# A hybrid attention, state-space and mixture-of-experts block: two places where work is put in another order

## The chip, the core and the metric

The kernel runs on one core of a Trainium2 chip. The metric is the time of one execution in microseconds (us) on the device; lower is better. The engines are TensorE (PE, matmuls; its weight loads stand apart as PEld), VectorE (DVE), ScalarE (ACT), GpSimd (POOL) and the queues from which DMAs are issued (SP, POOL and ACT). Each engine works through its own instructions in program order.

## The reference

A block takes 2048 tokens of 1024 channels and 16 meta tokens. After a LayerNorm it runs grouped-query attention (8 heads, 2 key heads, 64 wide) and a state-space layer side by side, gates and sums them, and normalizes. Then 16 experts each pick 256 tokens, work on them, and their results are added into the stream before a last LayerNorm.

```python
s = einsum('bqkgd,bskd->bkgqs', qblk, k) * scale
p = softmax(s, axis=-1)
o = einsum('bkgqs,bskd->bqkgd', p, v)
...
gate, idx = lax.top_k(softmax(logits, axis=1), cap)       # cap = 256 tokens for each expert
xe = t[idx]
h = silu(xe @ w_gate[e]) * (xe @ w_up[e])
ye = (h @ w_down[e]) * gate                               # added to the rows idx
...
h = layer_norm(alpha * h + moe, ln2_g, ln2_b)             # the output, 2048 rows
```

## The kernel before

**Attention** (`phase_b`). The work is 32 units: 4 blocks of 512 queries by 8 heads. A unit is 9 steps: 8 of 256 keys and a last one of the 16 meta keys. In a step PE makes scores (`scores`, tile `pS`), ACT takes the exponential (`pe`) and a 16-bit copy of it (`ph`, `split_hi`; for step 3 of a unit DVE makes that copy), POOL or DVE makes the 16-bit rest (`pl`, `split_lo`), and four steps later PE multiplies both with the values (`pv`, tile `po`).

The exponential needs the maximum of each row of scores beforehand. While one unit runs, PE makes plain scores of the next unit in 20 chunks of some 413 keys (`max_mm`, tile `pm`), and DVE reduces each chunk to a maximum per row (`max_red`, tile `mx`). When all 20 are reduced, `max_fin` joins them, and `max_put` has PE transpose them (four matmuls with the identity, again into a tile `pm`) and DVE copy the transposes into the rows 64 to 127 of the next unit's queries `q`. The tile `pm` has two buffers (PSUM banks). Chunks that wait for their reduction stand in the list `pend`; `red_all` reduces all of them.

What an engine does in a step follows a string, `PROG`, written out by hand: S and T are the two halves of the scores, M a chunk for the next unit, P a part of the values, and "/" means `red_all` and one item of DVE's queue. At a T the transposes are put too, where some are due:

```python
PROG=("SMTM/PPP/P/M/", "SMTMPP/PP/MM/M", "SMTM//PPPP/M/M")
```

**Experts** (`experts`). An expert is 16 steps: 8 halves of gate and up (`gate_up`, tile `pg`) and 8 of down (`down`, tile `pd`, two buffers). Weights come in pieces of 1 MB from SP's queue (tile `wr`, three buffers); ACT makes the rounded copy `wh` and DVE the rest `wl`. ACT and DVE also make the activation (`sg`, `hh`, `hl`), the transposed tokens (`xh`, `xl`) and, in the down steps, ACT moves each `pd` to `ye`. POOL's queue issues the gathers of tokens (`xg`) and the scatters that add `ye` to `acc_d` in memory.

**Final normalization.** From expert 9 on (`E0`) each step ends with `step(e, s)`, which takes every generator in `sides` one yield further. `finish` is the first of them: it loads two tiles of 128 rows of `acc_d` (`fx`, four buffers), and starts a pair of tiles every 11 steps through `norm`: sums of both tiles on ACT; one step later the mean on DVE (`fm`); then a square sum on ACT in each of two steps (`fj`, `fq`); a reciprocal root in two steps of small DVE instructions (`newton`); and four DVE steps that scale. Then POOL's queue stores the rows. `redo(e - 1)` starts in step 2 of each expert from 10 on: it gathers the rows that expert e - 1 changed (`fa`), and, five steps later, normalizes them in the same way and writes them over the output rows (`put_rows`). So `finish` and a `redo` run side by side, and in one step the job that stands first in `sides` has its instructions ahead on each engine.

Of the kernel before, what the change touches and what calls it, by code (L numbers as in the profile page):

```python
# [40 lines left out]
def row_bcast(ap, n, parts=128):  # L41
    return bass.AP(tensor=ap.tensor, offset=ap.offset, ap=[[0, parts], [1, n]])
# [7 lines left out]
def kernel(ctx, tc, x, meta, ln_in_g, ln_in_b, w_in, q_norm_g, k_norm_g,  # L50
# [326 lines left out]
    def phase_b(c):  # L377
# [61 lines left out]
        def load_q(n):  # L439
            qb, h = units[n]  # L440
            q1 = qp.tile([128, 512], F32R, name="q1", bufs=3)
            q2 = qp.tile([128, 512], F32R, name="q2", bufs=3)
            r, t0 = 64 * (h % 2), 512 * qb
            for i in range(2):
                SP.dma_start(f(q1[64 * i:64 * i + 64]), q_d[i, h // 2, r:r + 64, t0:t0 + 512])
            SP.dma_start(f(q2[:64]), q_d[0, h // 2, r:r + 64, t0:t0 + 512])
            Q[n] = q1, q2
            MX[n] = qp.tile([128, 4, 5], F32, name="mx")

        def max_mm(n, i):  # L450
            j, c = divmod(i, 5)
            k0, w = MC[c]
            p = po.tile([128, 512], F32, name="pm", bufs=2)
            PE.matmul(p[:, :w], Q[n][0][:, 128 * j:128 * j + 128], K1[units[n][1] // 4][:, k0:k0 + w],  # L454
                      start=True, stop=True)
            pend.append((n, j, c, p, w))
# [14 lines left out]
        def max_put(n):  # L471
            nm = NMT[n % 2]
            p = po.tile([128, 4, 128], F32, name="pm", bufs=2)
            for j in range(4):
                PE.matmul(p[:, j], nm[:, j], idr, start=True, stop=True)
            V.tensor_copy(Q[n][1][64:], p[64:].rearrange("p j q -> p (j q)"))  # L476

        def scores(n, i, a):
            g = units[n][1] // 4
            w = 2 if i < NT // 2 else 1  # L480
            m = 128 if i < NT // 2 else NM
            if a >= w:
                return
            if a == 0:
                PS[n, i] = ps.tile([128, 2, 512], F32, name="pS")
            p = PS[n, i]
            k0 = 128 * (2 * i + a)
            PE.matmul(p[:m, a], K2[g][:, k0:k0 + m], Q[n][1], start=True, stop=False)  # L488
            PE.matmul(p[:m, a], K1[g][:, k0:k0 + m], Q[n][0], start=False, stop=True)  # L489
            if a < w - 1:  # L490
                return
            e = pp.tile([128, 2, 512], F32, name="pe", bufs=PR["PE"]) if w == 2 else p[:, 1:]
            hi = pp.tile([128, 2, 512], F16, name="ph", bufs=PR["PH"])
            lo = pp.tile([128, 2, 512], F16, name="pl", bufs=PR["PH"])
            A.activation(e[:m, :w], p[:m, :w], AF.Exp, bias=ebias[:m], scale=HD ** -0.5)  # L495
            P[n, i] = e, hi, lo, m, w
# [5 lines left out]
        def split_hi(n, i, on_v):  # L502
            e, hi, lo, m, w = P[n, i]
            if on_v and i in PR["HI"]:
                V.tensor_reduce(hi[:m, :w], e[:m, :w, :, None], axis=AX.X, op=OP.max)  # L505
            if not on_v and i not in PR["HI"]:
                A.copy(hi[:m, :w], e[:m, :w])  # L507

        def split_lo(n, i):
            e, hi, lo, m, w = P[n, i]  # L510
            (PL if w == 2 else V).tensor_tensor(lo[:m, :w], e[:m, :w], hi[:m, :w], op=OP.subtract)  # L511
# [27 lines left out]
        def pv_fin(n):  # L539
            qb, h = units[n]  # L540
            if h == 0:
                Y[qb] = sm.tile([128, 4, 512], F32, name="y")
            y = Y[qb]
            t = O.pop(n).rearrange("p a b d -> p (a b) d")
            r = sm.tile([128, 4], F32, name="r")
            V.reciprocal(r, t[:, :, 64])
            PL.tensor_tensor(t[:, :, 0:64], t[:, :, 0:64], t[:, :, 65:129], op=OP.add)
            PL.tensor_tensor(y[:, :, 64 * h:64 * h + 64], t[:, :, 0:64],
                             r[:, :, None].to_broadcast([128, 4, 64]), op=OP.mult)
            if h == H - 1:  # L550
                PL.dma_start(y_d[512 * qb:512 * qb + 512].rearrange("(j p) d -> p j d", p=128), y)
# [6 lines left out]
        def red_all():  # L558
            while pend:
                n, j, c = pend[0][:3]  # L560
                max_red()
                if (j, c) == (3, 4):
                    max_fin(n)
                    put.append(n)
# [30 lines left out]
        for s in range(len(steps) + LAG):  # L595
            want = min(NC, int((s + LEAD) * 20 // NP))
            live = s < len(steps)
            if live:
                n, i = steps[s]
                if i == 0 and n + 2 < NU:  # L600
                    load_q(n + 2)
            if 0 <= s - PR["LOS"] < len(steps) and steps[s - PR["LOS"]][1] < NP - 1:
                split_lo(*steps[s - PR["LOS"]])
            if 0 < s <= len(steps) and steps[s - 1][1] in PR["HI"]:
                vq.insert(0, lambda st=steps[s - 1]: split_hi(*st, True))
            if fin and fin[0][0] == s:
                vq.append(lambda x=fin.pop()[1]: pv_fin(x))
            if s >= LAG:
                pvq += [(*steps[s - LAG], k) for k in range(4)]
            prog = PR["PROG"][s % len(PR["PROG"])]  # L610
            if s == len(steps) + LAG - 1:
                prog = prog.replace("P", "") + "P/" * len(pvq)
            for tok in prog:
                if tok == "M" and done < want:
                    if len(pend) == 2:
                        red_all()
                    max_mm(*chunks[done])
                    done += 1
                elif tok == "S" and live:
                    scores(n, i, 0)  # L620
                elif tok == "T":
                    if live:
                        if n and i == 0:
                            vq.pop(0)()
                        scores(n, i, 1)
                    while put:
                        max_put(put.pop())
                elif tok == "P" and pvq:
                    u, k, part = pvq.pop(0)
                    pv(u, k, part)  # L630
                    if (k, part) == (NP - 1, 3):
                        pv_out(u)
                        fin.append((s + 2, u))
                elif tok == "/":
                    red_all()
                    if vq:
                        vq.pop(0)()
            if live:
                split_hi(n, i, False)
                if i == NP - 1:  # L640
                    vq.insert(0, lambda st=steps[s]: split_lo(*st))
            if s == len(steps) - 1:
                c2.close()
            if s == len(steps) + LAG - 1:
                while vq:
                    vq.pop(0)()
            yield "tail" if s >= len(steps) else "pre" if s == len(steps) - 40 else ""
# [1033 lines left out]
    def experts(c, pos, inf):  # L1681
# [221 lines left out]
        def finish():  # L1903
            SP.dma_start(gb, row_bcast(ln2_g, D))
            SP.dma_start(bb, row_bcast(ln2_b, D))
            xs = {}

            def load(t):
                xs[t] = fp.tile([128, D], F32, name="fx", bufs=4)
                PL.dma_start(xs[t], acc_d[128 * t:128 * t + 128])  # L1910

            yield
            for t in range(2):
                load(t)
            yield
            yield

            def base(t):
                for n, _ in enumerate(norm([xs[t], xs[t + 1]])):
                    if n == 7 and t + 2 < NT:  # L1920
                        load(t + 2)
                        load(t + 3)
                    yield
                for i in range(2):
                    PL.dma_start(outs[t + i], xs.pop(t + i))

            yield from pipe((base(t) for t in range(0, NT, 2)), every=MO[3])
# [11 lines left out]
        sides = []  # L1939

        def step(e, s):
            if (e, s) == (E0, 0):
                sides.append(finish())
            if E0 < e < E - 1 and s == MO[0]:
                sides.append(redo(e - 1, MO[1]))
            if (e, s) == (E - 1, 1):
                acc_rows(e)
                sides.append(redo(e - 1, MO[2]))
            for g in sides:
                next(g, None)  # L1950

        one_hot(0, 0, NT)
# [188 lines left out]
```

## Time and profile before

| | |
|---|---|
| time, median of 3 runs | 3164.24 us (3161.82 to 3164.74) |
| profiled execution, its own time | 3164.63 us |
| its span, first to last instruction | 3162.1 us |
| PE busy | 2969.1 us (94%) |
| DVE busy | 2162.1 us (68%) |
| ACT busy | 1549.6 us (49%) |
| POOL busy | 1007.6 us (32%) |
| mean granted TensorE clock | 0.977 |

The 2.5 us between the span and its execution's time lie outside the instructions. Busy shares are means over stages: in attention ACT and POOL are nearly full, in the experts they are not.

### The profile page before, as it was taken

How to read it: one execution, taken by the hardware profiler on the slowest of the kernel's cores; microseconds unless marked ns; L12 is line 12 of the kernel's file. 1: busy time of each engine (PE TensorE's matmuls, PEld its weight loads, DVE VectorE, ACT ScalarE, POOL GpSimd, SP SyncE). 2: the span in 40 equal slices, each digit the busy share in tenths (PEclk: the TensorE clock that was granted, in tenths of full speed). 3: DMA queues.
4: the chain of work that ended last, by engine and by line, in shares of the span. 5: the costliest groups of instructions: out<-in, count | busy, mean ns of one | idle time of the engine just before them, and what ended most of it. 6: DMA issues, size and time to landing. Idle time of an engine off the chain costs nothing.

```text
span 3162.1 us, 56209 instructions
## 1 busy us (share of the span) xinstructions
PE 2969.1 (94%) x22829; PEld 2632.9 (83%) x22829; DVE 2162.1 (68%) x3760; ACT 1549.6 (49%) x2197; POOL 1007.6 (32%) x630
## 2 busy tenths in 40 slices
PE   7998999999989999999899996799999999999997
PEld 6887797777867777777678885699999999999997
DVE  7885689683377777776466666666666665778786
ACT  2222352233358888888522222344444444655553
POOL 2221035051069999998510001111111101122221
PEclk9999999999999999999999998799999999999999
DMA  6566633557510101013366643466677667778784
GB/s 234 183 202 201 151 97 114 183 146 198 178 41 22 35 21 35 21 35 89 111 207 197 200 134 107 137 210 214 211 224 219 213 214 238 255 261 270 263 264 156
DMA packets 464498, 513.00 MB, mean 162 GB/s; under 512 B 47568, under 2 KB 387728, under 8 KB 463856
## 3 DMA queue, kind: packets, MB, share of 16 engines
q1 hardware_dynamic: 433616, 421.20, 42.6%
q0 software_dynamic: 19232, 69.53, 7.2%
q10 hardware_dynamic: 11392, 18.68, 1.7%
q8 instruction: 179, 2.93, 0.4%
q14 instruction: 79, 0.65, 0.1%
HBM read 385.59 MB, written 123.76 MB: 161 GB/s over the span
## 4 chain that ended last, share of the span: by engine, by line
PE 67%; DVE 14%; DMA 7%; issue 5%; ACT 4%; SPq 1%; POOL 1%; ACTq 0%; POOLq 0%; DVEq 0%
PE pg L1794 17%; PE pd L1822 7%; PE pg L1240 7%; PE po L529 6%; PE pw L1393 5%; PE pb L1325 5%; PE pm L454 4%; PE pS L488 4%; PE pS L489 4%; DVE wl L1702 1%; PE pz L1157 1%; ACT wh L1701 1%; DMA acc_d<-ye,ix 1%; DMA wr<-in_w_down_e_dram 1%; PE pB L944 1%
## 5 line engine op out<-in xcount | busy, mean ns | idle before, releaser
L1794 PE MATMUL pg<-xh,wh 128*128 128x256 f32 x2048 | 573.6, 280 | 6.8 <-DVE sg L1802 5.5
L1702 DVE TENSOR_TENSOR wl<-wr,wh 128x2048 fp32r<-128x2048 f32 x189 | 433.1, 2291 | 205.2 <-ACT wh L1701 205.1
L1794 PE MATMUL pg<-xh,wl 128*128 128x256 f32 x2048 | 570.9, 279 | 2.2 <-DVE wl L1702 2.2
L1794 PE MATMUL pg<-xl,wh 128*128 128x256 f32 x2048 | 571.1, 279 | 0.0
L511 POOL TENSOR_TENSOR pl<-pe,ph 128x1024 f16<-128x1024 f32 x256 | 544.6, 2147 | 59.9 <-DVE ph L505 44.9
L460 DVE TENSOR_REDUCE mx<-pm 128x1 f32<-128x412 f32 (+1 forms) x640 | 362.5, 583 | 137.4 <-PE pm L454 124.9
L1794 PEld LDWEIGHTS pg<-xh,wh 128*128 128x128 f32 x2048 | 386.8, 189 | 7.8 <-DVE sg L1802 6.0
L1794 PEld LDWEIGHTS pg<-xh,wl 128*128 128x128 f32 x2048 | 386.0, 188 | 2.9 <-DVE wl L1702 2.8
L1794 PEld LDWEIGHTS pg<-xl,wh 128*128 128x128 f32 x2048 | 386.7, 189 | 0.0
L1701 ACT CAST wh<-wr 128x2048 fp32r<-128x2048 f32 x189 | 359.6, 1903 | 14.9 <-DMA wr<-in_w_up_e_dram 8.7
L1240 PE MATMUL pg<-gh,gwh 128*128 128x512 f32 x1024 | 335.0, 403 | 23.3 <-ACT gg L1211 16.6
L495 ACT ACTIVATE pe<-pS,ebias 128x1024 f32<-128x1024 f32 x256 | 284.4, 1111 | 53.1 <-PE pS L489 53.1
L1822 PE MATMUL pd<-wh,hh 128*128 128x256 f32 x1024 | 286.8, 280 | 6.8 <-ACT ye L1841 4.3
L1822 PE MATMUL pd<-wh,hl 128*128 128x256 f32 x1024 | 284.9, 278 | 1.8 <-DVE hl L1809 1.8
L1822 PE MATMUL pd<-wl,hh 128*128 128x256 f32 x1024 | 284.2, 277 | 0.0
L454 PE MATMUL pm<-k,q 128*128 128x412 f32 (+1 forms) x640 | 231.4, 371 | 30.7 <-DVE q L476 23.6
L1240 PEld LDWEIGHTS pg<-gh,gwh 128*128 128x128 f32 x1024 | 193.9, 192 | 66.0 <-ACT gg L1211 19.4
L529 PEld LDWEIGHTS <-ph 128*128 128x128 f16 (+1 forms) x2176 | 192.7, 97 | 63.7 <-issue 60.5
L507 ACT CAST ph<-pe 128x1024 f16<-128x1024 f32 x224 | 234.4, 1046 | 17.8 <-ACT pe L495 0.4
L529 PE MATMUL po<-v,ph 128*128 128x129 f16 (+1 forms) x2176 | 241.5, 222 | 0.4 <-ACT t L536 0.4
L488 PE MATMUL pS<-q,k 128*128 128x512 f32 (+1 forms) x544 | 232.8, 428 | 0.9 <-DVE q L476 0.8
L1844 POOL DMA_INDIRECT acc_d<-ye,ix x30 | 69.2, 2308 | 471.6 <-ACT ye L1841 457.5
(424 smaller groups left out, 6895.9 us busy)
## 6 DMA issues: line engine op xcount, KB each, us to landing
wr<-in_w_gate_e_dram SPq DMA_DIRECT2D x64, 1024.0 KB
wr<-in_w_up_e_dram SPq DMA_DIRECT2D x64, 1024.0 KB
wr<-in_w_down_e_dram SPq DMA_DIRECT2D x64, 1024.0 KB
gwr<-in_w_in_dram SPq DMA_DIRECT2D x32, 512.0 KB
gh<-ht_d SPq DMA_DIRECT2D x64, 256.0 KB
gt_d<-gg ACTq DMA_DIRECT2D x64, 256.0 KB
gt<-gt_d SPq DMA_DIRECT2D x32, 512.0 KB
q<-q_d SPq DMA_DIRECT2D x96, 128.0 KB
```

Of the source, the lines that this page charges most:

```text
L454: PE.matmul(p[:, :w], Q[n][0][:, 128 * j:128 * j + 128], K1[units[n][1] // 4][:, k0:k0 + w], start=True, stop=True)
L460: V.tensor_reduce(MX[n][:, j, c:c + 1], p[:, :w], axis=AX.X, op=OP.max)
L488: PE.matmul(p[:m, a], K2[g][:, k0:k0 + m], Q[n][1], start=True, stop=False)
L495: A.activation(e[:m, :w], p[:m, :w], AF.Exp, bias=ebias[:m], scale=HD ** -0.5)
L507: A.copy(hi[:m, :w], e[:m, :w])
L511: (PL if w == 2 else V).tensor_tensor(lo[:m, :w], e[:m, :w], hi[:m, :w], op=OP.subtract)
L529: PE.matmul(o[:, 0:nc_], pt_[:m, a, 128 * j:128 * j + 128], v16[:m, kt, g, 0:nc_], start=(kt == 0 and j % 2 == 0 and x == 0), stop=(last a ...
L1240: PE.matmul(p, w[:, k], h, start=(k == 0 and j == 0), stop=(k == 7 and j == 2))
L1701: A.copy(wh, wr)
L1702: V.tensor_tensor(wl, wr, f(wh), op=OP.subtract)
L1794: PE.matmul(p[:, gu], w[:, k, cs_], x[:, k], start=(k == 0 and j == 0), stop=(k == 7 and j == 2))
L1822: PE.matmul(p, a[:, k, cs_], w[:, k], start=(k == 0 and j == 0), stop=(k == 7 and j == 2))
```

## The change

Three edits. In attention, where transposes of the row maxima are due, the chunks that wait in `pend` are reduced ahead of them. In `finish`, five steps lie between the first load and its use, where two did, and the store of a pair comes one step later. In `step`, the generators are taken in reversed order, so that the one that started last has its instructions ahead.

```diff
                         scores(n, i, 1)
                     while put:
+                        red_all()
                         max_put(put.pop())
...
             for t in range(2):
                 load(t)
-            yield
-            yield
+            for _ in range(5):
+                yield
...
                         load(t + 2)
                         load(t + 3)
                     yield
+                yield
                 for i in range(2):
                     PL.dma_start(outs[t + i], xs.pop(t + i))
...
-            for g in sides:
+            for g in reversed(sides):
                 next(g, None)
```

DVE, attention, where a unit's maxima are joined (`nm`) and copied into the next unit's queries (`q_8382`); a row with x5 stands for five instructions in succession. PE's and SP's order is the same in both kernels.

```order
 L467 TENSOR_REDUCE nm_7900<-mx 128x4
 L469 TENSOR_REDUCE nm_7900<-m_8923 128x4
-L460 TENSOR_REDUCE mx<-pm 128x1
+L460 TENSOR_REDUCE mx<-pm 128x1 x2
 L476 CAST q_8382<-pm 64x512
-L460 TENSOR_REDUCE mx<-pm 128x1 x5
+L460 TENSOR_REDUCE mx<-pm 128x1 x4
 L511 TENSOR_TENSOR pl<-pS,ph 16x512
 L460 TENSOR_REDUCE mx<-pm 128x1 x11
```

One reduction has moved from behind the copy of the transposes to ahead of it. The same piece stands 30 times in the difference, once for each of the units 1 to 30.

ACT, expert 9, the first sums of `fx`, before: they stand behind the third `hh` of the expert's gate and up steps.

```order
L1808 CAST hh<-sg 128x256
L1884 ACTIVATE fj,fm<-fx 128x1024 x2
L1800 ACTIVATE sg<-pg 128x256
L1701 CAST wh<-wr 128x2048
L1808 CAST hh<-sg 128x256
```

And now, three steps later, in the step before the tokens of the next expert (`xh`) are taken over:

```order
L1809 CAST hh<-sg 128x256
L1885 ACTIVATE fj,fm<-fx 128x1024 x2
L1801 ACTIVATE sg<-pg 128x256
L1702 CAST wh<-wr 128x2048
L1782 CAST xh<-pt 128x4x128 x2
```

Three more `gate_up` steps now lie between the loads and this first use; every later pair of `fx` is three steps later too.

ACT, expert 11, its last gate and up step and the first down steps (`fa` are the rows of `redo`, `ye` what the down steps wait for), before:

```order
L1890 ACTIVATE fj,fq<-fx,fm 128x1024
L1884 ACTIVATE fj,fm<-fa 128x1024 x2
L1800 ACTIVATE sg<-pg 128x256
L1781 CAST xh<-pt 128x4x128 x2
L1808 CAST hh<-sg 128x256
L1701 CAST wh<-wr 128x2048
L1841 ACTIVATE ye<-pd,gv 128x256
L1890 ACTIVATE fj,fq<-fa,fm 128x1024
L1841 ACTIVATE ye<-pd,gv 128x256
L1701 CAST wh<-wr 128x2048
L1890 ACTIVATE fj,fq<-fa,fm 128x1024
L1841 ACTIVATE ye<-pd,gv 128x256 x2
```

And now:

```order
L1885 ACTIVATE fj,fm<-fa 128x1024 x2
L1885 ACTIVATE fj,fm<-fx 128x1024 x2
L1801 ACTIVATE sg<-pg 128x256
L1782 CAST xh<-pt 128x4x128 x2
L1809 CAST hh<-sg 128x256
L1702 CAST wh<-wr 128x2048
L1842 ACTIVATE ye<-pd,gv 128x256
L1891 ACTIVATE fj,fq<-fa,fm 128x1024
L1891 ACTIVATE fj,fq<-fx,fm 128x1024
L1842 ACTIVATE ye<-pd,gv 128x256
L1702 CAST wh<-wr 128x2048
L1891 ACTIVATE fj,fq<-fa,fm 128x1024
```

The sums of the next pair have taken the place of a square ahead of `sg`, and squares of that pair stand between the `ye` of the first down steps. In expert 12 it is the other way round: there the pair's sums stood between two `ye` with a square of `fa` and a `wh`, and now they stand three steps later.

## Rows read from the trace of the kernel before

**Rows 1.** Busy time, granted clock and DMA in windows: attention, the experts 8, 9 and 12, 20 us.

```profile
core 0: us, PE busy (x) PEld busy (x) DVE busy (x) ACT busy (x) POOL busy (x), PEclk, DMA share, GB/s
895.00:1513.00 618.00, 591.65 (x5940) 480.76 (x5939) 437.26 (x868) 537.60 (x585) 558.87 (x308) 0.99 0.11 34
...
2501.83:2570.00 68.17, 68.17 (x630) 68.14 (x627) 43.29 (x61) 32.89 (x42) 7.97 (x4) 1.00 0.70 217
...
2638.20:2714.60 76.40, 71.67 (x630) 71.25 (x628) 49.85 (x83) 40.58 (x56) 10.16 (x10) 0.96 0.73 237
...
2860.70:2935.30 74.60, 71.70 (x629) 71.27 (x626) 59.87 (x117) 44.40 (x61) 18.17 (x14) 0.98 0.80 266
...
2660.00:2680.00 20.00, 15.27 (x110) 15.07 (x108) 10.49 (x14) 12.52 (x19) 0.00 (x0) 0.83 0.54 191
```

**Rows 2.** Who waited for the copy of the transposes, L476 (us, times).

```profile
  PEld pm L454: 27.9, 30
  PE pm L454: 23.6, 30
```

**Rows 3.** PE's timeline in one unit: start, us, instruction, idle before and releaser.

```profile
952.55 0.35 PE L454 MATMUL pm<-k,q 128*128 128x414 f32 x1
...
953.20 0.56 PE L475 MATMUL pm<-idr,nm 128*128 128x128 f32 x4
954.55 0.46 PE L454 MATMUL pm<-k,q 128*128 128x412 f32 x1 [0.79 <-DVE q L476]
```

**Rows 4.** DVE's timeline in the same unit.

```profile
951.86 0.58 DVE L460 TENSOR_REDUCE mx<-pm 128x1 f32<-128x414 f32 x1
953.80 0.69 DVE L476 CAST q<-pm 64x512 fp32r<-64x512 f32 x1 [1.36 <-PE pm L475]
```

**Rows 5.** POOL's timeline in the same unit.

```profile
952.58 14.87 POOL L511 TENSOR_TENSOR pl<-pe,ph 128x1024 f16<-128x1024 f32 x7
969.00 2.14 POOL L511 TENSOR_TENSOR pl<-pe,ph 128x1024 f16<-128x1024 f32 x1 [1.55 <-DVE ph L505]
```

**Rows 6.** ACT's timeline: its waits of that unit.

```profile
956.22 0.64 ACT L495 ACTIVATE pS<-pS,ebias 16x512 f32<-16x512 f32 x1 [0.37 <-PE pS L489]
...
958.68 1.12 ACT L495 ACTIVATE pe<-pS,ebias 128x1024 f32<-128x1024 f32 x1 [1.16 <-PE pS L489]
```

**Rows 7.** PE's timeline in the experts 9, 11, 11, 12, 13.

```profile
2665.25 0.58 PE L1794 MATMUL pg<-xh,wh 128*128 128x256 f32 x1 [4.73 <-DVE sg L1802]
...
2838.88 0.39 PE L1822 MATMUL pd<-wh,hh 128*128 128x256 f32 x1 [0.73 <-ACT ye L1841]
...
2857.51 0.38 PE L1794 MATMUL pg<-xh,wl 128*128 128x256 f32 x1 [1.23 <-DVE wl L1702]
...
2916.96 0.58 PE L1822 MATMUL pd<-wh,hh 128*128 128x256 f32 x1 [2.65 <-ACT ye L1841]
...
2977.43 1.25 PE L1772 MATMUL pt<-idf,xg 128*128 128x128 f32 x8 [1.28 <-DVE xl L1782]
```

**Rows 8.** ACT's timeline in the experts 9, 11, 12, 12, 12, 13.

```profile
2661.35 1.06 ACT L1884 ACTIVATE fj<-fx 128x1024 f32<-128x1024 f32 x1 [9.12 <-DMA fx<-acc_d]
...
2837.22 1.15 ACT L1890 ACTIVATE fj<-fa,fm 128x1024 f32<-128x1024 f32 x1 [4.00 <-DVE fm L1886]
...
2909.64 1.15 ACT L1890 ACTIVATE fj<-fa,fm 128x1024 f32<-128x1024 f32 x1 [3.72 <-DVE fm L1886]
...
2912.95 1.06 ACT L1884 ACTIVATE fj<-fx 128x1024 f32<-128x1024 f32 x1
...
2915.30 1.15 ACT L1890 ACTIVATE fj<-fa,fm 128x1024 f32<-128x1024 f32 x1
...
2967.85 1.06 ACT L1884 ACTIVATE fj<-fx 128x1024 f32<-128x1024 f32 x1 [2.09 <-DMA fx<-acc_d]
```

**Rows 9.** DMA issues of the page: the final stores, KB each, median us to landing.

```profile
out_dram<-fx POOLq DMA_DIRECT2D x16, 512.0 KB, 4.7
```

**Rows 10.** POOL's timeline: the first put of the rows of expert 13.

```profile
3074.93 1.78 POOL L1900 DMA_INDIRECT out_dram<-fa,io  x1 [14.79 <-DVE fa L1897]
```

## The prediction

> **What bounds the kernel now.** I read the windows by stage first. In attention PE is busy for 591.65 of 618 us, so 26.35 us of it are idle [rows 1]. POOL and ACT are busy for 558.87 and 537.60 us: PE leads, and both others are close behind it. Then I asked who waits for what. Nearly all of PE's idle time in attention has one releaser: the copy of the transposes, L476, kept PE waiting 30 times, 23.6 us in sum, and its weight loads 27.9 us [rows 2]. The timelines of one unit show how. A chunk of plain scores runs at 952.55 and ends at 952.90; the transposes run from 953.20 to 953.76; the next chunk starts at 954.55, after 0.79 us of idle time [rows 3]. DVE meanwhile had finished the reduction before at 952.44 and waited 1.36 us for the transposes; the copy took 0.69 us, until 954.49 [rows 4]. The new chunk went into the bank that the transposes left, since the other one still held a chunk that nobody had reduced. So DVE stood idle while a full bank waited for it.
>
> In the experts PE is the bound too, and an undisturbed expert (the eighth) takes 68.17 us with no idle time. Expert 9, the first with the final normalization beside it, takes 76.40 and expert 12 takes 74.60 [rows 1]. PE's timeline there has single waits of 0.7 to 4.73 us [rows 7], and ACT's timeline says what came before them: it waited 9.12 us for the first `fx` [rows 8], did no `sg` meanwhile, and PE ran out of free `pg`.
>
> **Part 1, the reduction ahead of the transposes.** It removes nothing: DVE's instructions are the same, one of 0.58 us stands earlier, 30 times. The chunk ends at 952.90, so its reduction would end at about 953.48, 0.28 us before the transposes end at 953.76 [rows 3, 4]. The copy then starts when it did, at 953.80, and the next chunk finds the reduced bank free as soon as PE comes to it. The 0.79 us go. The idle time of the weight load is larger (27.9 / 30 = 0.93 us), as a matmul's successor starts ahead of the end that the timeline gives it; the truth lies between 30 x 0.79 = 23.6 and 30 x 0.93 = 27.9 us [rows 2]. I take **27 us**, near the upper end, since PE's next matmul could overlap the last transpose.
>
> What is late next? The chunk after that needs the bank of the copy, free at 954.49 as before, and comes in the next step. POOL works without a pause for most of a unit (seven `pl` in 14.87 us) and then waits 1.55 us, once in each unit [rows 5]. ACT waits 0.37 and 1.16 us, 1.53 us together [rows 6]. A unit that is 0.93 us shorter leaves each about 0.6 us. So both still fit, by little; without that cover, what goes over 1.53 us would be lost.
>
> A rule of the Trainium skill speaks against this gain. "Perfetto Trace Analysis", section "Optimization Strategy", says of consistent bubbles, the same gap repeated over a stretch, that they can mean too few SBUF or PSUM buffers for the next tile. By it two banks stay two banks, the gap stays, and this part gives nothing instead of 27 us. The trace agrees that the bank is what is missing, but shows it full and idle.
>
> **Part 2, five steps from load to use.** The wait of 9.12 us on ACT goes: three steps of about 5.5 us (an undisturbed expert's 68.17 us hold eight of these and eight of half their length: 68.17 / 12 = 5.7 at most) are over 16 us, more than the wait. With it goes PE's wait of 4.73 us [rows 7]. The granted clock was 0.83 in the 20 us with and behind that wait, so part of it at the lower of its two levels, 1.2 GHz; that is worth 0.17 x 20 = 3.4 us more [rows 1]. Together **8.1 us**, close to 76.40 - 68.17 = 8.2.
>
> The shift also moves every later pair of tiles against the other work of ACT:
> - Expert 12: the pair's sums (2912.95 to 2915.30, 2.35 us) stood with a square (1.15 us) between two `ye`, and PE waited 2.65 us for the second [rows 7, 8]; the clock of that expert was 0.98, 0.02 x 74.60 = 1.5 us [rows 1]. The sums are now three steps later, alone. Gain 0 to 4.1, I take **4.1**.
> - Expert 13: ACT waited at 2967.85 for an `fx` again (2.09 us, the second of its pair) [rows 8], and PE 1.28 us for what ACT did next [rows 7]. Now five steps lie between, and the sums come in the down steps. Gain 0 to 1.3, I take **1**.
> - Expert 11: the sums of a pair (2.35 us) take the place of a square (1.15) ahead of `sg`, and two squares more stand between the first `ye`: 2.35 - 1.15 + 2 x 1.15 = 3.5 us of ACT, in a place where PE waited 0.73 us already. Against it the sums that stood in this expert's last step, and with them the wait of 1.23 us for `wl`, go elsewhere [rows 7, 8]. Cost 3.5 - 1.2 = **2.3 us**; between -1.2 (ACT's share hidden) and 5.0 (all of it, and 1.5 us of clock as in expert 12).
>
> **Part 3, stores a step later and the youngest job first.** The instructions stay. In the first down steps ACT waited 4.00 and 3.72 us for the mean `fm` of a redo, which stood behind an `fx` instruction on DVE [rows 8]; now it stands ahead of it. That is part of what frees expert 12 and is not counted again. A store later on POOL's queue has the next redo's first put behind it, which writes the same output; behind that stand the scatter, the last gathers and all of the end. The last store moves from four steps ahead of the put of expert 13 to one. The put waited 14.79 us for its rows until 3074.93 [rows 10], and a store takes 4.7 us to land [rows 9], against down steps of some 2.8 us: it may be some 2 us late. Cost 0 to 3, I take **1**.
>
> **Sum.** -27 - 8.1 - 4.1 - 1 + 2.3 + 1 = -36.9 us, on the profiled execution's own 3164.63 us: 3127.7, say 3128. That execution lies 0.4 us above the median of the runs shown, so no correction is needed. All best ends give about -27.9 - 8.1 - 4.1 - 1.3 - 1.2 = -42.6 (3122); with all of expert 12's 6.4 us over 68.17 gone too, 3120. All worst ends give -23.6 - 8.1 + 5 + 3 = -23.7 (3141).
>
> **Rivals.**
> - A, the final part gives its gain back: the pair's sums and squares meet the redo's in the down steps of experts 10, 11 and 13, and each costs what expert 12 lost, 4.1 us. 12.3 us on 3128 give 3140, up to 3150 with expert 9's share lost too. For it: redo and `finish` have periods of 16 and 11 steps and must meet somewhere. Against it: five steps remove two of ACT's waits for transfers.
> - B, the bubble stays, because the next chunk now waits for the moved reduction: only the final part's 10 us come, 3155. For it: the margin is 0.28 us [rows 3, 4]; the skill's rule above says the same. Against it: a chunk that waits for a reduction begun at 952.9 still starts a microsecond before 954.55.
> - C, POOL or ACT becomes the bound of attention: half of the 27 us, 3141. For it: only 0.6 us left in each; against it: none of the two has to be earlier than now in its own step.
> - D, slower or no change: in all five experts 10 to 14 the younger job's instructions and the three steps pile ACT's work ahead of `sg` or `ye`, so that PE stands long enough to lose its clock, as in expert 9, 8.1 us each. 40.5 us against the sum give 3168. It decides above 36.9 / 5 = 7.4 us for each expert. Against it: the pile in expert 12 cost 4.1, and no other was as high.
>
> **How the numbers follow.** The forecast has 0.66 (its own range 3120 to 3138), A 0.17, B 0.08, C 0.05, D 0.04. The range 3119 to 3143 holds the forecast, C and more than half of A, some 0.8. Faster by over 0.2% (6.3 us; about what a measurement here can tell) are the forecast, A, C and 0.07 of B: 0.95. Within 0.2%: 0.01 of B and half of D, 0.03. Slower: 0.02.
>
> **What would show it.** In attention: L476 releases no PE wait; a unit lasts about 18.9 us and POOL's wait in it is about 0.6 us; the stage is some 27 us shorter. If L460 stands as the releaser of PE's wait instead, it is B. In expert 9: no wait of ACT for `fx`, a granted clock of 1.00, some 68 to 70 us. In expert 12: the wait of 2.65 us gone; in expert 11 a longer one at the first `ye`. The put of expert 13 behind a store that has not landed would show the cost of part 3. The prediction is wrong if the chunk behind the transposes waits for something that these rows hide behind the copy, or if the final part's waits move to experts that had none.

## The result, and the profile after

The changed kernel takes 3127.88 us (median of 4 runs, 3123.30 to 3135.52), against 3164.05 us before: a ratio of 0.9889, 95% interval 0.9867 to 0.9911. The forecast was 3128 us. Its profiled execution took 3125.16 us, with a span of 3123.3 us, 38.8 us less than before.

The windows by stage, after. The bounds of an expert are PE's first matmuls of two successive `pick`s; these are attention, from its first to its last transposes, and the experts 9 to 13.

```profile
core 0: us, PE busy (x) PEld busy (x) DVE busy (x) ACT busy (x) POOL busy (x), PEclk, DMA share, GB/s
888.50:1479.10 590.60, 586.14 (x5927) 478.37 (x5926) 441.42 (x869) 533.77 (x584) 555.06 (x308) 0.99 0.12 36
...
2607.30:2675.50 68.20, 68.20 (x626) 68.14 (x624) 50.02 (x82) 37.33 (x48) 11.30 (x10) 1.00 0.78 248
2675.50:2746.00 70.50, 70.50 (x627) 70.44 (x626) 55.80 (x102) 45.99 (x64) 13.04 (x10) 1.00 0.80 266
2746.00:2819.40 73.40, 70.67 (x627) 69.84 (x625) 58.38 (x116) 41.93 (x56) 14.53 (x13) 1.00 0.78 254
2819.40:2898.60 79.20, 73.67 (x627) 72.80 (x626) 59.57 (x105) 44.36 (x62) 17.54 (x18) 0.96 0.82 270
2898.60:2968.00 69.40, 68.65 (x626) 68.27 (x624) 58.47 (x115) 44.09 (x59) 14.21 (x12) 1.00 0.83 267
```

The same windows of before, attention between the same bounds and expert 11, which [rows 1] did not have:

```profile
892.40:1511.70 619.30, 592.16 (x5926) 481.29 (x5926) 438.84 (x869) 536.30 (x584) 557.57 (x308) 0.99 0.11 34
...
2784.60:2860.20 75.60, 71.54 (x626) 70.11 (x624) 61.25 (x106) 44.13 (x60) 21.36 (x17) 1.00 0.83 275
```

Attention is 28.7 us shorter, expert 9 by 8.2, expert 11 by 2.2, expert 13 by 3.6 us (all of before are in the table below). Expert 12, where the forecast had a gain, is 4.6 us **longer** (79.20 against 74.60 in [rows 1]). The rest nearly cancels: work ahead of attention, which is the same in both, happened to end 3.9 us earlier, the stretch between attention and expert 9 is 2.3 us longer, the last two experts 0.7.

**Attention.** Who waited for the copy L476 in attention, after (us, times); [rows 2] had 27.9 and 23.6 us here:

```profile
L476 DVE CAST q<-pm x32: 694/694/696, 888.8 to 1479.4; 64x512 fp32r<-64x512 f32 x32
...
who waited for it (us, times):
  PEld pS L488: 0.9, 1
  PE pS L488: 0.8, 1
```

No chunk waits for the copy any more. In one unit, PE's timeline answers to [rows 3], DVE's to [rows 4], POOL's to [rows 5]:

```profile
946.04 0.35 PE L454 MATMUL pm<-k,q 128*128 128x414 f32 x1
...
946.69 0.56 PE L475 MATMUL pm<-idr,nm 128*128 128x128 f32 x4
947.09 0.43 PE L454 MATMUL pm<-k,q 128*128 128x412 f32 x1
```

The weight load of that last chunk:

```profile
947.07 0.19 PEld L454 LDWEIGHTS pm<-k,q 128*128 128x128 f32 x1
```

```profile
946.43 0.59 DVE L460 TENSOR_REDUCE mx<-pm 128x1 f32<-128x414 f32 x1 [0.50 <-PE pm L454]
947.29 0.69 DVE L476 CAST q<-pm 64x512 fp32r<-64x512 f32 x1 [0.27 <-PE pm L475]
```

```profile
961.55 2.14 POOL L511 TENSOR_TENSOR pl<-pe,ph 128x1024 f16<-128x1024 f32 x1 [0.72 <-DVE ph L505]
```

The reduction runs from 946.43 to 947.02, beside the transposes; the next chunk starts 0.40 us after the first of them (1.35 us before, 953.20 to 954.55) and overlaps the last. That is 0.95 us a unit, a little above the forecast's 0.79 to 0.93. POOL's pause fell from 1.55 to 0.72 us: it still fits.

**Expert 12.** ACT's timeline, after: its three long waits for weights there.

```profile
2841.78 1.91 ACT L1702 CAST wh<-wr 128x2048 fp32r<-128x2048 f32 x1 [2.70 <-DMA wr<-in_w_gate_e_dram]
...
2850.97 1.91 ACT L1702 CAST wh<-wr 128x2048 fp32r<-128x2048 f32 x1 [5.55 <-DMA wr<-in_w_up_e_dram]
...
2859.10 1.92 ACT L1702 CAST wh<-wr 128x2048 fp32r<-128x2048 f32 x1 [4.51 <-DMA wr<-in_w_down_e_dram]
```

The wait of 2.65 us for `ye` [rows 7] is gone, as forecast. In its place 12.8 us of ACT's time went into waiting for weights, which the sum did not have at all. PE then waited for what DVE makes behind ACT's copies, first for `wl`, then for `xl`:

```profile
2855.25 0.58 PE L1795 MATMUL pg<-xh,wl 128*128 128x256 f32 x1 [1.83 <-DVE wl L1703]
...
2868.80 1.97 PE L1773 MATMUL pt<-idf,xg 128*128 128x128 f32 x8 [2.68 <-DVE xl L1783]
```

Of the 4.6 us, 2.6 are idle time of PE (79.20 - 73.67 against 74.60 - 71.70) and 2.0 are busy time, with a granted clock of 0.96 instead of 0.98.

### The profile page after: what moved, and what is told of

Its sections match the earlier page's. It is cut to its first block, busy times and chain, and to the rows that moved or that the text cites. A ratio compares the mean times of both kernels' runs of the same rounds, so it can differ in the third digit from the quotient of the medians.

```text
span 3123.3 us, 56215 instructions
## 1 busy us (share of the span) xinstructions
PE 2960.4 (95%) x22829; PEld 2628.3 (84%) x22829; DVE 2165.8 (69%) x3760; ACT 1547.7 (50%) x2197; POOL 1003.3 (32%) x630
## 4 chain that ended last, share of the span: by engine, by line
PE 70%; DVE 12%; DMA 6%; issue 5%; ACT 4%; POOL 1%; SPq 1%; ACTq 0%; POOLq 0%; DVEq 0%
PE pg L1795 19%; PE pd L1823 9%; PE pg L1241 7%; PE po L529 6%; PE pw L1394 6%; PE pb L1326 5%; PE pm L454 4%; PE pS L488 4%; PE pS L489 4%; PE pz L1158 1%; PE pB L945 1%; DMA gh<-ht_d 1%; DVE wl L1703 1%; DMA acc_d<-ye,ix 1%; PE pt L1773 1%
## 5 line engine op out<-in xcount | busy, mean ns | idle before, releaser
L460 DVE TENSOR_REDUCE mx<-pm 128x1 f32<-128x412 f32 (+1 forms) x640 | 365.1, 584 | 138.0 <-PE pm L454 124.6
L1845 POOL DMA_INDIRECT acc_d<-ye,ix x30 | 59.8, 1992 | 517.7 <-ACT ye L1842 496.0
```

Source lines behind the costliest of these rows:

```text
L460: V.tensor_reduce(MX[n][:, j, c:c + 1], p[:, :w], axis=AX.X, op=OP.max)
```

## The experiments

All edits below are against the changed kernel. The times of the experts, from the profiled execution of each kernel (us, one trace each; in kernels whose experts are the same the experts 9 to 13 repeat within 2 us, with one exception named below, and the last two within 5):

| kernel | 9 | 10 | 11 | 12 | 13 | 10 to 13 | 14 and 15 |
|---|---|---|---|---|---|---|---|
| before | 76.4 | 70.5 | 75.6 | 74.6 | 73.1 | 293.9 | 135.3 |
| the change | 68.2 | 70.5 | 73.4 | 79.2 | 69.5 | 292.5 | 136.0 |
| attention only | 76.3 | 70.5 | 80.1 | 73.2 | 72.6 | 296.5 | 135.0 |
| final part only | 68.2 | 70.5 | 73.4 | 79.4 | 70.0 | 293.2 | 137.4 |
| the change again | 68.2 | 70.5 | 73.4 | 78.8 | 71.2 | 293.9 | 140.6 |
| reduction twice | 68.2 | 70.3 | 73.4 | 78.5 | 70.1 | 292.2 | 137.5 |
| five steps alone | 68.2 | 70.8 | 73.4 | 78.2 | 73.5 | 295.9 | 138.0 |
| store not later | 68.2 | 70.5 | 74.0 | 78.8 | 69.5 | 292.8 | 139.1 |
| old order of jobs | 68.2 | 70.9 | 73.4 | 73.6 | 70.8 | 288.6 | 140.5 |
| two steps again | 74.9 | 72.9 | 72.4 | 75.5 | 72.0 | 292.8 | 136.5 |
| transfers alone | 68.2 | 70.1 | 70.1 | 73.5 | 68.2 | 281.9 | 135.6 |
| work alone | 68.2 | 69.7 | 73.4 | 70.4 | 69.5 | 283.0 | 134.9 |
| pairs apart | 68.2 | 70.3 | 70.1 | 69.5 | 68.2 | 278.0 | 146.0 |
| pairs together | 68.2 | 73.4 | 76.3 | 77.6 | 78.0 | 305.2 | 152.6 |

**The two halves of the change.** The final part undone (the last three pieces of its diff), then the attention part undone, and the changed kernel once more beside them.

```diff
-            for _ in range(5):
-                yield
+            yield
+            yield
...
-                yield
                 for i in range(2):
                     PL.dma_start(outs[t + i], xs.pop(t + i))
...
-            for g in reversed(sides):
+            for g in sides:
```

> Only the reduction ahead of the transposes; the final part as before. If the two parts add up, this gives attention's share of the gain: 30 units of 0.93 to 0.95 us, some 28 us, so a time of about 3136 us, and experts 9 to 13 as long as before (76.4, 70.5, 75.6, 74.6, 73.1 us). If attention's faster pace also shifts the weights' loads in the experts, the expert times change although nothing was edited there.

```diff
                     while put:
-                        red_all()
                         max_put(put.pop())
```

> Only the final part's three edits; attention as before. If the parts add up: some 8 to 10 us less than before, 3154 to 3156 us, with 8.2 us of it in expert 9, and the 0.79 us idle times behind the transposes in place. Rival: the final part gives back in expert 12 (79.2 us against 74.6 in the traces at hand) all that it gains elsewhere, and this kernel stands within 3 us of before.

> The changed kernel once more, since its runs so far spread over 12 us (3123.3 to 3135.5) and those of before over 3. If the spread comes from the experts' transfers, a second trace shows experts 10 to 14 with other times than 70.5, 73.4, 79.2 and 69.5 us, and attention with the same 590.6 us between the first and the last transposes. If it comes from attention, that stage differs.

Measured, with before at 3161.93 us beside them: attention alone 3136.19 us, ratio 0.9924 (0.9910 to 0.9939); the final part alone 3158.27, 0.9988 (0.9978 to 0.9997, so 1 to 7 us); the whole change 3132.33, 0.9904 (0.9890 to 0.9919). The halves add up: 25.7 + 3.7 = 29.4 us against 29.6. So attention gave what it was priced at, and the final part 3.7 us (3.9 by the difference of the first kernel and the third), not the 9.9 us of the sum.

One stage did not stay where it was expected: with attention alone expert 11 took 80.1 us, against 75.6 before, though nothing is edited in the experts. ACT waited there 2.91, 6.01 and 2.10 us for weights, and 2.15 and 3.05 us before. So the same order of work can cost 4.5 us more in another execution, and a difference of that size in one expert of one trace shows little by itself. In that trace expert 11, where the pair met the redo before, was as dear as expert 12 is in the change (79.2 us).

**The moved reduction made twice.** A second, useless reduction of the same chunk stands between the first and the copy.

```diff
+        def red_twice():
+            again = list(pend)
+            red_all()
+            while again:
+                n, j, c, p, w = again.pop(0)
+                V.tensor_reduce(MX[n][:, j, c:c + 1], p[:, :w], axis=AX.X, op=OP.max)
...
-                        red_all()
+                        red_twice()
```

> The changed kernel with the moved reduction made twice, so that the bank comes free some 0.55 us later; the result is the same. If the next chunk now waits for nothing but that reduction, with 0.1 to 0.3 us to spare, PE's idle time comes back in part, 0.3 to 0.5 us in each of 30 units: 9 to 15 us slower than the changed kernel, 3137 to 3143 us, and L460 or its twin as the releaser. Rival: PE has a microsecond to spare here and the extra reduction is hidden: no more than 2 us.

It took 3143.75 us, 0.9945 (0.9932 to 0.9957), 11.4 us over the change beside it. Attention in its trace lasts 608.2 us, 17.6 us over the change: 0.59 us for each of 30 units, all of the added instruction (0.589 us). (The whole span grew by 8.7 us only: the stretch behind attention was 4.4 us shorter in this execution, the experts 10 to 15 by 4.8.) PE's waits for the second reduction, L563, and one of them in the timeline:

```profile
  PEld pm L454: 17.6, 30
  PE pm L454: 13.4, 30
```

```profile
952.08 0.45 PE L454 MATMUL pm<-k,q 128*128 128x412 f32 x1 [0.44 <-DVE mx L563]
```

The chunk behind the transposes starts 0.05 us after the reduction (951.44 to 952.03) and 30 times out of 30 waits for it, not for the copy, which starts only at 952.06. That shows which bank it takes: the reduced chunk's. Some 0.3 to 0.5 us a unit were expected, since a margin was counted on; it took the whole 0.59.

**Which piece of the final part does what.** My theory was now that the later store made expert 12's loss. Four kernels: the store back in its step and the old order of the jobs (first and second piece), the store alone back, the old order alone, two steps again (third piece).

```diff
-                yield
                 for i in range(2):
                     PL.dma_start(outs[t + i], xs.pop(t + i))
...
-            for g in reversed(sides):
+            for g in sides:
...
-            for _ in range(5):
-                yield
+            yield
+            yield
```

> The attention edit and the five steps; the store is back in its old step and the generators are in their old order. My theory: the five steps alone bring expert 9's 8.2 us (68.2 us, no wait of ACT for fx); the loss of expert 12 (79 us against 74.6 before) comes from the later store, which puts the stores, the loads and the redo's gathers into the same steps as the weights' pieces. Then expert 12 takes 73 to 75 us here and the time is some 4 us below the whole change, ratio 0.987 to 0.989. Rival: the loss comes from the three steps of shift themselves, which put the pair's work beside the redo's; then expert 12 takes 78 us or more here too, and the time is that of the whole change, ratio 0.989 to 0.991.

> The whole change with the store back in its old step. My theory (the later store makes the loss of expert 12): expert 12 takes 71 to 75 us, ratio 0.987 to 0.989. Rival (the three steps make it): 78 us or more, ratio about 0.990, as the whole change. If the reversed order is what hurts, expert 12 takes 78 us or more here and not in the kernel with five steps alone.

> The whole change with the generators in their old order. My theory (the later store makes the loss of expert 12): 78 us or more in expert 12, ratio about 0.990. The prediction had the younger job's mean ahead of the older job's squares as part of what frees expert 12: by that this kernel's ACT waits some 4 us for the mean of a redo again in experts 11 and 12, and it is up to 4 us slower than the whole change.

> The whole change with two steps from load to use again, as before. Theory of the prediction: expert 9 goes back to 76.4 us (its 8.2 us hang on the five steps alone) with a wait of ACT of some 9 us for fx. Expert 12: if the later store alone makes its loss, 78 us or more; if the three steps make it, 70 to 75 us. So either 3140 (8 us above the whole change) or 3135 (4 us above).

Measured, in this order, with before at 3164.84 us: 3134.86 us, 0.9907 (0.9893 to 0.9920); 3127.53, 0.9882 (0.9865 to 0.9898); 3130.79, 0.9891 (0.9876 to 0.9907); 3134.73, 0.9901 (0.9887 to 0.9915). The intervals overlap, so the totals rank none of the four; the stages tell more. Expert 9 goes back to 74.9 us with two steps (76.4 expected), and only then; ACT's wait for the first `fx` is back in that kernel:

```profile
2632.35 1.06 ACT L1885 ACTIVATE fj<-fx 128x1024 f32<-128x1024 f32 x1 [7.66 <-DMA fx<-acc_d]
```

So the five steps alone bring expert 9's gain. My theory on expert 12 **fell**: with the store in its old step it takes 78.2 and 78.8 us. (With two steps it takes 75.5, between the two forecasts.) The old order of the jobs alone gives 73.6, in one trace. POOL's queue shows what differs. In the change, the loads of a pair stand behind a put of the redo:

```profile
2817.78 1.86 POOL L1901 DMA_INDIRECT out_dram<-fa,io  x1 [41.10 <-DVE fa L1898]
2819.64 1.09 POOL L1911 DMA_DIRECT2D fx<-acc_d  x2
```

With the old order of the jobs they stand ahead of it, and go out 35 us ahead of expert 12, which begins at 2821.0 (in the change 0.2 us behind its start):

```profile
2785.74 0.54 POOL L1911 DMA_DIRECT2D fx<-acc_d  x1 [7.20 <-DMA out_dram<-fx]
...
2820.61 5.58 POOL L1901 DMA_INDIRECT out_dram<-fa,io  x1 [32.69 <-DVE oh L1734]
```

With five steps alone the loads are early too, but the stores stand between two puts, and since all write the output each waits for the one ahead to land; the gathers of the next redo come last:

```profile
2827.51 1.16 POOL L1926 DMA_DIRECT2D out_dram<-fx  x2 [3.99 <-DMA out_dram<-fa,io]
2837.26 2.74 POOL L1901 DMA_INDIRECT out_dram<-fa,io  x1 [8.59 <-DMA out_dram<-fx]
...
2853.89 0.98 POOL L1857 DMA_INDIRECT fa<-acc_d,ix  x1 [7.56 <-DMA acc_d<-ye,ix]
```

There ACT waits 4.44 us for `fa` and not for weights:

```profile
2859.53 1.06 ACT L1885 ACTIVATE fj<-fa 128x1024 f32<-128x1024 f32 x1 [4.44 <-DMA fa<-acc_d,ix]
```

The kernel with the store not later has its loads behind the put, as the change has, and still loses like this one, at `fa` and with no wait for a weight above 0.4 us:

```profile
2866.34 1.06 ACT L1885 ACTIVATE fj<-fa 128x1024 f32<-128x1024 f32 x1 [5.51 <-DMA fa<-acc_d,ix]
```

So there are two ways to lose the same 5 us. The changed kernel takes the first: late loads together with late stores. With the stores in their old step the loss is the second, wherever the loads stand.

**Transfers or work.** The first job (`finish`) without its sums, squares and scaling; then with them, but without its transfers.

```diff
-                for n, _ in enumerate(norm([xs[t], xs[t + 1]])):
+                for n in range(9):
```

> The whole change, but the final normalization's first job only moves its rows: the loads and stores stand in their steps, its sums, squares and scaling are left out, so the rows that no redo writes are stored as they were loaded. My theory (expert 12 loses time because the pair's load and store meet the redo's transfers and the weights): expert 12 still takes 76 to 80 us, experts 10 to 13 together 287 to 293 us (292.5 in the whole change). Rival (ACT's and DVE's work of the pair makes it): expert 12 takes 70 to 72 us, the four together 278 to 283 us.

```diff
-            for t in range(2):
+            for t in range(4):
                 load(t)
...
-                for n, _ in enumerate(norm([xs[t], xs[t + 1]])):
-                    if n == 7 and t + 2 < NT:
-                        load(t + 2)
-                        load(t + 3)
+                for n, _ in enumerate(norm([xs[t % 4], xs[t % 4 + 1]])):
                     yield
                 yield
-                for i in range(2):
-                    PL.dma_start(outs[t + i], xs.pop(t + i))
```

> The whole change, but the first job's transfers are left out: it loads four tiles once, in expert 9, works on them again and again, and stores nothing, so most output rows are written by no one. My theory (the transfers): expert 12 takes 70 to 72 us, experts 10 to 13 together 279 to 284 us, no wait of ACT for a weight or a gathered row over 1 us in expert 12. Rival (the work): 77 to 80 us and 288 to 293 us.

The windows of expert 12 with transfers alone, and of the experts 11 and 12 with work alone:

```profile
2811.30:2884.80 73.50, 71.33 (x627) 70.97 (x626) 49.97 (x83) 37.59 (x48) 15.62 (x15) 0.98 0.86 283
```

```profile
2744.40:2817.80 73.40, 70.80 (x626) 69.97 (x624) 59.09 (x117) 41.90 (x56) 15.43 (x9) 1.00 0.70 225
2817.80:2888.20 70.40, 69.52 (x626) 69.27 (x624) 59.76 (x105) 44.34 (x62) 18.08 (x10) 1.00 0.76 244
```

The work alone behaves as my theory said (70.4 us in expert 12, 283.0 in sum). The transfers alone do not: 73.5 us, where I had 76 to 80, and the sum of 281.9 is the rival's. In expert 12 the transfers alone cost some 3 us over the 70.1 of the experts 10 and 11, the work alone next to nothing, both together 9: the transfers are needed for the loss, but it takes ACT's work beside them to make it that large. Expert 11 is the other way round: 73.4 us with work alone, 70.1 with transfers alone. Its loss in the change is ACT's pile.

**Where the pairs meet the redo.** The pairs begin every 11 steps and the redo every 16, so the place at which they meet moves. The redo's puts, scatters and gathers stand from step 14 of an expert to step 2 of the next. Counted from expert 9, a pair that starts in step s loads the next one in s + 7 and stores in s + 10 (s + 9 before). Before, a load and a store stood in steps 32 and 34, the start of expert 11; now in 46 and 49, around the start of expert 12. Two kernels set the starts by hand: one keeps them out of that place in experts 10 to 13, the other puts them there each time.

```diff
-            yield from pipe((base(t) for t in range(0, NT, 2)), every=MO[3])
+            act, n = [], 6
+            for t, s in zip(range(0, NT, 2), (6, 17, 28, 44, 60, 76, 87, 98)):
+                while n < s:
+                    act = [g for g in act if next(g, 0) is None]
+                    yield
+                    n += 1
+                act.append(base(t))
+            while act:
+                act = [g for g in act if next(g, 0) is None]
+                yield
```

The second has 6, 23, 39, 55, 71, 82, 92, 102 in place of these starts.

> The whole change with the pairs begun at other steps: counted from expert 9, the eight pairs start in steps 6, 17, 28, 44, 60, 76, 87, 98 and not in 6, 17, 28, 39, 50, 61, 72, 83. Then in experts 10 to 13 no load or store of a pair falls between step 14 of an expert and step 2 of the next, where the redo's puts, the scatters and the gathers stand. My theory: experts 10 to 13 take 70 to 71.5 us each, 280 to 286 together, and the time is 3 to 10 us below the whole change, 3118 to 3126, ratio 0.986 to 0.988. Against it: one pair now meets that place behind expert 14, and the last store comes 15 steps later, which may cost up to 5 us in the last two experts. Rival (the sum of the losses is set by the number of bytes or of instructions, not by where they meet): 290 to 294 us together, no gain.

> The opposite: the pairs start in steps 6, 23, 39, 55, 71, 82, 92, 102, so that in each of the experts 10 to 13 a load falls in step 14 and a store in step 1 of the next expert, as they do once in the whole change, around the start of expert 12. My theory: experts 11, 12 and 13 take 77 to 80 us each, experts 10 to 13 together 302 to 310 us, the time is 10 to 20 us above the whole change (part of it is the last pair's, which ends behind the last expert). Rival (number of bytes or instructions): 290 to 296 us together.

The experts 10 to 13, first with the pairs apart, then together (in this last kernel the last pair is stored behind a redo's rows, so some output rows hold older values):

```profile
2679.10:2749.40 70.30, 70.30 (x627) 70.20 (x625) 55.59 (x101) 45.98 (x64) 12.84 (x10) 1.00 0.79 266
2749.40:2819.50 70.10, 70.10 (x627) 70.06 (x626) 57.95 (x103) 41.91 (x56) 17.65 (x14) 1.00 0.85 278
2819.50:2889.00 69.50, 69.50 (x628) 69.47 (x627) 56.48 (x102) 41.69 (x56) 18.62 (x12) 1.00 0.81 265
2889.00:2957.20 68.20, 68.20 (x628) 68.16 (x627) 56.60 (x102) 41.95 (x56) 15.88 (x13) 1.00 0.86 278
```

```profile
2679.20:2752.60 73.40, 70.58 (x627) 69.75 (x626) 50.31 (x97) 41.72 (x56) 8.76 (x6) 1.00 0.68 224
2752.60:2828.90 76.30, 71.45 (x627) 69.86 (x625) 56.69 (x102) 42.15 (x56) 19.17 (x13) 1.00 0.76 249
2828.90:2906.40 77.50, 72.05 (x626) 70.83 (x624) 56.20 (x102) 42.03 (x56) 17.22 (x13) 0.98 0.76 244
2906.40:2984.40 78.00, 71.56 (x627) 69.82 (x626) 56.33 (x102) 42.05 (x56) 16.65 (x13) 1.00 0.75 243
```

Apart: 278.0 us, 14.5 less than the change and better than the 280 to 286 expected; PE has no pause. Together: 305.2 us, inside the 302 to 310 expected, and ACT's waits are those of expert 12 in the change (in its expert 13 they are 2.83, 5.92 and 3.03 us for weights). What the queues moved in 32 us of expert 12, POOL's (q0) and SP's, which has the weights (q1), MB in the middle; first the change (2830 to 2862, DMA share 1.03), then the pairs apart (2831 to 2863, 0.98):

```profile
q0 software_dynamic: 1568, 5.70, 53.2%
q1 hardware_dynamic: 5040, 5.09, 49.1%
```

```profile
q1 hardware_dynamic: 6265, 6.32, 58.4%
q0 software_dynamic: 1164, 4.19, 39.1%
```

The 16 DMA engines are about as busy in both; what POOL's queue moved more, the weights' queue moved less.

The totals, with before at 3163.27 us: apart 3125.18 us, 0.9871 (0.9851 to 0.9891); together 3165.51, 0.9999 (0.9986 to 1.0011); transfers alone 3115.97, 0.9845 (0.9821 to 0.9869); work alone 3114.36, 0.9838 (0.9814 to 0.9863). "Together" is slower than I expected (10 to 20 us over the change), since its last two experts lose 16.6 us against the change as well. "Apart" has the lowest time of the kernels that compute everything, but not by more than its interval. It gives 10 us back in the last two experts, where ACT waits for the gathers of the last redo (6.53 us, 1.57 us in the change):

```profile
3065.29 1.06 ACT L1885 ACTIVATE fj<-fa 128x1024 f32<-128x1024 f32 x1 [6.53 <-DMA fa<-acc_d,ix]
```

## Why the prediction was right, and where it was not

**Part 1 was right in mechanism and size.** 27 us were forecast; the traces show 28.7 (the change) and 26.7 us (attention only), the timed runs 25.7. L476 releases none of these waits, a unit takes 18.9 us, POOL's wait fell to 0.72 us. The margin of 0.28 us (0.23 in the trace, 947.02 to 947.25) was counted to the end of the transposes, but the chunk overlaps the last of them and does not wait for that end: its weight load starts 0.05 us after the reduction in all 30 units, with one reduction as with two. So nothing was to spare, and a second reduction cost all of its 0.59 us. Whether PE could have come sooner, had the reduction ended earlier still, no run shows.

**Rival B had the order right and the price wrong.** The next chunk does start on the moved reduction's end, but the trace has no idle time of PE ahead of it. The Trainium skill ("Perfetto Trace Analysis", section "Optimization Strategy") says that a gap that repeats can mean too little room for the next tile, by the number of buffers or the size of the tiles. This case's traces do not bear that out: PE's gap of 0.79 us (0.93 at the weight load) went in all 30 units with two banks as before.

**Expert 9 was right:** 8.2 us measured, 8.1 forecast, no wait for `fx`, a clock of 1.00. The kernel with two steps shows that the five steps do it.

**Expert 12 had the wrong sign:** "Gain 0 to 4.1, I take 4.1", and it lost 4.6 us. The step that failed is in part 3: it counted the stores that move on POOL's queue, and took the new order for help to ACT (the wait for `fm`), but did not count the loads. With the younger job first, the loads stand behind its put, which waits 41.10 us, and with the store a step later they meet the scatters, gathers and stores around the start of expert 12. In the old order expert 12 takes 73.6 us, although ACT there waits 3.71 us for `fm`, as before [rows 8].

**Expert 11:** a cost of 2.3 us was forecast, a gain of 2.2 came. The pile on ACT was sized well: 73.4 us against 70.1 without the work, 3.3 us where 3.5 stood. What was missing is that the pair's transfers had left this expert. Before, ACT waited there 2.15 and 3.05 us for weights; in the change it waits for none there, and for 12.8 us in expert 12. Against the kernel with attention alone the gain is 6.7 us (80.1 to 73.4), so its size is uncertain.

**Expert 13** gained 3.6 us, not 1: PE's idle time there fell by 2.0 us (2.8 to 0.75), and the other 1.7 are busy time at a clock of 1.00 in both traces, which the sum did not have. **The last two experts** lost 0.7 us in the profiled execution, where 1 was forecast, but not for the reason given: the put of expert 13 (3038.06) waited 4.05 us for its own rows, not for a store. The same program run again lost 5.3 us there, so the 0.7 says nothing.

So rival A was in part true: the final part gave 3.7 us of its 9.9, because jobs with periods of 11 and 16 steps "must meet somewhere". Its mechanism was not what it named (sums and squares in the down steps): without the pair's transfers the loss of expert 12 is not there, and ACT's work beside them makes it larger. That the total fell on the forecast to 0.2 us was luck. By the runs beside each other the change is worth 29.6 us, not 36.9; the same program's second median, 3132.33 us, lies in the range too, but 4 us above the forecast.

That the weights on SP's queue are late when POOL's transfers pile up agrees with the Trainium skill ("DMA: Bandwidth & Descriptors", section "Issuing engines are not separate DMA queues"): transfers from all issuing engines run on the same 16 DMA engines and interleave. The traces agree: at a DMA share of 1.03 POOL's queue moved 5.70 MB and SP's 5.09, against 4.19 and 6.32 where the pairs stand apart.

**Open:** why transfers and work together cost 9 us in expert 12 where each alone costs some 3 or less was not taken apart further. With the transfers alone, the queues moved about the same in such a stretch (6.30 and 5.22 MB, share 1.03) and ACT had one wait for weights, 3.32 us, so full DMA engines are not the whole of it. Of the 9 us, 5.5 are idle time of PE, and the rest is busy time with the granted clock at 0.96 (0.98 with transfers alone, 1.00 with work alone). It was not tried to keep the pairs apart and finish them by the step in which the change does, which might keep both gains.

## What to carry to other kernels

If a stage has a repeating gap, ask first which buffer is full, and whether the engine that frees it is idle: here an instruction moved ahead of another freed it, with no buffer added. When two jobs with different periods share a DMA queue, list for every load and store the step in which it is issued and what it stands behind; moving one job only moves the place where they meet, and what one expert gains another loses until their starts keep them apart. An order of jobs that helps one engine changes the order on every queue.

## What the runs showed of the hardware

The same matmuls have two paces at a granted clock of 1.00. In expert 15 a step of gate and up took 5.44 us in the change and 5.65 or 5.72 us when the same program ran again, seen at ACT's `sg`. First the change, then the change again, each with its window:

```profile
3051.82 0.39 ACT L1801 ACTIVATE sg<-pg 128x256 f32<-128x256 f32 x1 [3.01 <-PE pg L1795]
3057.26 0.39 ACT L1801 ACTIVATE sg<-pg 128x256 f32<-128x256 f32 x1 [2.95 <-PE pg L1795]
```

```profile
3051.80:3068.20 16.40, 16.40 (x147) 16.40 (x146) 10.41 (x12) 7.53 (x10) 6.84 (x5) 1.00 1.04 342
```

```profile
3046.70 0.39 ACT L1801 ACTIVATE sg<-pg 128x256 f32<-128x256 f32 x1 [3.37 <-PE pg L1795]
3052.35 0.39 ACT L1801 ACTIVATE sg<-pg 128x256 f32<-128x256 f32 x1 [3.17 <-PE pg L1795]
```

```profile
3046.60:3063.80 17.20, 17.20 (x148) 17.20 (x147) 10.66 (x13) 7.52 (x10) 4.84 (x3) 1.00 0.97 268
```

PE is busy all the time in both. Both paces also stand in one execution: in the change a step takes 5.44 us in expert 9 and 5.65 in expert 10, so expert 10 takes 70.5 us and not 68.2, though PE is busy for all of it. So a difference of some 2 us between two experts need not come from a wait. Between the two executions the last two experts differ by 4.6 us (136.0 and 140.6), of which 3.4 are busy time of PE, expert 13 by 1.7 and attention by 0.1. What sets the pace was not found; it is part of why totals of one program differ by 4 us.
